# Hybrid encoder trunk on one core: the Hyena DFT in half blocks and plain float32

## The chip, the cores and the metric

The kernel runs on one core of a Trainium2 chip. The metric is device time in microseconds (us). PE is TensorE, with its weight loads as PEld; DVE is VectorE, ACT is ScalarE, POOL is GpSimd, and SP is SyncE, whose queue issues nearly all DMAs.

## What is computed

One layer of an encoder, for a prompt of 512 rows and a sample of 2048 rows of 1024 numbers. A normed input is projected onto three groups of heads (mLSTM, retention, Hyena), each is gated, and the output product and a final norm follow. The change touches only the Hyena group and its filters:

```python
def long_conv(u, spec, skip):
    l = u.shape[1]
    y = irfft(rfft(u, n=2 * l, axis=1) * spec[None], n=2 * l, axis=1)[:, :l]
    return y + u * skip

def hyena_branch(hy_in, hy_z, conv_w, conv_b, spec, skip):
    u = centred_conv3(hy_in, conv_w, conv_b)
    v, x1, x2 = split(u)                     # 512 channels each
    z = x1 * long_conv(v, spec[:, 0], skip[0])
    z = x2 * long_conv(z, spec[:, 1], skip[1])
    return z * silu(hy_z)
```

`spec` is the spectrum of a two-sided filter of the sequence's doubled length, made by a small sine network and a decay window, and normed by its absolute sum.

## The kernel before

A transform of length N (1024 or 4096) is two stages of matmuls. With n = 64 n1 + n2, the first stage (`stage_a0`, `stage_a`) transforms over n1, the second, one frequency k1 at a time (`freq`), over n2; the way back has the same two, the second of them in `inv_a`. Between the stages the data lie in DRAM (`Sg`, `F`, `Z`), since each stage has other numbers in its partitions. All tiles are 128 partitions by 512 channels.

Accuracy of float32 comes in one of two ways. `split` makes two float32r parts of an operand, a rounded one on ACT and a remainder on DVE or POOL, and `mm3` does three matmuls of parts. A matmul of float32 tiles needs no parts.

- **Stage over n1** (`stage_a`): the 128 partitions of a tile hold GS (the number of n2 values) interleaved short transforms; the matrix `ai` is 128x128 for each half h, block diagonal with interleaved blocks, so half of its rows are zero for a half h. Two `mm3` per tile, 20 tiles per order.
- **Frequency step** (`freq`): per k1 it loads a constant tile `cB` (forward and inverse matrix), a signal tile and a filter tile. `front` splits all three, `muls` does an `mm3` for each of signal and filter and swaps partition halves by DMAs, `mid` multiplies the complex numbers on DVE and POOL and splits the product, `back` does the `mm3` of the inverse. 40 steps per order, two orders.
- **Inverse stage** (`inv_a`): two loads, two splits and two `mm3` per tile that add into one PSUM tile; the gate product follows, and in order 0 at once the next order's `stage_a`.
- **Filters** (`filters`): per tile `first` (an `mm3`, the window), `product`, `total`/`second` (sums), `third` (a plain float32 matmul with the 128x128 matrix `fa`), `store`. 40 tiles per order.

The work around is woven in by hand: generators yield a cost on PE and a due time, and `merge` takes next the stream that is furthest behind its share (`lag` gives the due time). In the merge of `run`, the chain of Hyena stages runs beside the projections of the Hyena columns and the retention heads. `hb` is a ring of 9 tiles (HB), `hp` one of 16 (2 x HP) for parts; CB and FB are rings of constants and filter tiles. The mLSTM heads and the final product come behind. L numbers are lines of this kernel.

Of the kernel before, what the change touches and what calls it, by code (L numbers as in the profile page):

```python
# [39 lines left out]
HB, HP, CB, FB, B1, B2, KA, KB, KC, LS2, WF, VB, FH = 9, 8, 3, 3, 5, 6, 3, 3, 1, 3, 70, 4, 8  # L40
# [14 lines left out]
def fft_consts(L):  # L55
# [13 lines left out]
    FA = np.zeros((128, 128))  # L69
    for l in range(GF):  # L70
        FA[l::GF, l::GF] = A
    HG = GS // 2
    SA = np.zeros((128, 2, 128))
    IA = np.zeros((128, 2, 128))
    for h in range(2):
        for l in range(HG):
            n2l = h * HG + l
            SA[n2l::GS, h, l::HG] = A[:V]
            IA[l::HG, h, n2l::GS] = IAm
# [25 lines left out]
def constants():  # L105
    C = {'ident': np.eye(128, dtype=np.float32)}
    feats, tneg = [], []
    for L in (LP, LS):
# [9 lines left out]
        for j in range(NTF):  # L118
            n = 64 * (p // GF) + (p % GF) * (64 // GF) + j
# [27 lines left out]
class Trunk:  # L147
# [62 lines left out]
    def run(self):  # L210
        tc = self.tc
        with ExitStack() as ctx:
# [4 lines left out]
            with ExitStack() as c1:  # L217
# [5 lines left out]
                with tc.tile_pool(name="hy", bufs=2, side="right") as self.hy:  # L223
                    self.ai_of = (0, None)
                    self.drain(self.merge((self.chain(self.stage_a0(), self.freq(0), self.inv_a(0), self.freq(1), self.inv_a(1)), 270 * W3),
                                          (self.chain(self.projections(), self.retention()), 848)))
# [339 lines left out]
    def filter_setup(self):  # L566
# [4 lines left out]
        for L in (LP, LS):  # L571
            self.fa[L] = self.T(p0, [128, 128], f"FA{L}", bufs=1)
            nc.sync.dma_start(self.fa[L], C[f'FA{L}'])

    def filter_weights(self, o):
# [3 lines left out]
        raw, dl = self.T(p0, [128, 512], "fo"), self.T(p0, [128, 512], "dl", bufs=1)  # L579
# [42 lines left out]
    def filters(self, o):  # L622
# [11 lines left out]
        def first(n):  # L634
# [11 lines left out]
            if j == 0:  # L646
                sk[L] = self.T(p0, [128, 512], "fo")[0:1]
# [46 lines left out]

        n = len(seq)
        for i in range(n + 2):
            if i < n:
                first(i)
            if 0 <= i - 2:
# [6 lines left out]
            if 0 <= i - 2:  # L706
# [5 lines left out]
    def filter_mlp(self, i, blk):  # L712
# [20 lines left out]
        xv = x.rearrange("p (t c) -> p t c", t=4)  # L733
        outs = [(hd[0:64, :, 0:64], xv[0:64, :, 0:64]), (hd[64:128, :, 64:128], xv[64:128, :, 64:128])]
        if b == 0:
            outs.append((hd[64:128, 0, 0:1], xv[64:128, 0, 0:1]))
        self.sin(pm, outs, x, 128)
        if b == 0:
            nc.gpsimd.memset(hd[64:128, 0, 64:65], 0.0)
# [24 lines left out]
    def fetch_ai(self, L):  # L764

        if self.ai_of[0] != L:
            raw = self.hb().rearrange("p (a b) -> p a b", a=4)
            self.nc.sync.dma_start(raw, self.C[f'AI{L}'])
            self.ai_raw = (L, raw)

    def ai(self, L):

        if self.ai_of[0] != L:
            assert self.ai_raw[0] == L
            hl = [self.T(self.hy, [128, 4, 128], f"ai{i}", F32R, bufs=1) for i in range(2)]
            self.split(*hl, self.ai_raw[1])
            self.ai_of = (L, hl)
        return self.ai_of[1]
# [101 lines left out]
    def parts(self, t, eng=None):  # L880
        return self.split(*(self.T(self.hy, [128, 512], "hp", F32R, bufs=HP) for _ in range(2)), t, eng=eng)

    def stage_a0(self):
# [3 lines left out]
        def load(i):  # L887
            L, j = seq[i]
            st[i] = self.hb(self.X[0][L][j])

        n = len(seq)
        self.fetch_ai(LP)
        load(0)
        load(1)
        for i in range(n + 1):
            if i:
                L, j = seq[i - 1]
                self.stage_a(L, 0, j, st.pop(i - 1))
                if i < n and seq[i][0] != L:
                    self.fetch_ai(seq[i][0])  # L900
            if i < n:
                st[i] = self.parts(st[i])
                self.ai(seq[i][0])
            if i + 2 < n:
                load(i + 2)
            yield self.lag(1.28, 2.0)
# [12 lines left out]
    def freq(self, o):  # L919
# [5 lines left out]
        raw, As, Cs, X, Y = {}, {}, {}, {}, {}  # L925

        def load(i):
            L, k = seq[i]
            c = self.T(hy, [128, 256], "cB", bufs=1)
# [7 lines left out]
        def front(i):  # L937
            c, a, f = raw.pop(i)
            Cs[i] = self.split(*[self.T(hy, [128, 256], f"cB{x}", F32R, bufs=CB) for x in range(2)], c, eng=nc.gpsimd)
            As[i] = self.parts(a), self.parts(f, nc.gpsimd)  # L940

        def muls(i):

            (a, f), c, k = As.pop(i), [x[:, 0:128] for x in Cs[i]], seq[i][1]
# [6 lines left out]
            self.mm3(pf, c, f)  # L951
# [12 lines left out]
        def mid(i):  # L964
# [20 lines left out]
        for i in range(-1, n + 1):  # L985
            if i + 1 < n:
                front(i + 1)
# [14 lines left out]
    def inv_a(self, o):  # L1002
# [4 lines left out]
        def load(i):  # L1007
            L, j = seq[i]
            zs[i] = [self.hb(self.Z[L, o][:, 32 * h + j:32 * h + 32:geo(L)['NTS'], :]) for h in range(2)]

        def load_x(i):
            L, j = seq[i]
            xs[i] = self.hb(self.X[o + 1][L][j]), self.hb(self.hyg[SEQ0[L] + j:SEQ0[L] + L:geo(L)['NTS'], :]) if o == 1 else None

        def front(i):
# [717 lines left out]
```

## Time and profile before

| | |
|---|---|
| runs | 2694.83, 2703.0, 2709.08 us, median 2703.0 |
| profiled execution | 2704.09 us, span 2702.3 us |
| mean granted TensorE clock | 0.98 of full speed |
| DMA | 364.24 MB, mean 135 GB/s |
| instructions | 47221, of them 17590 matmuls |

The span is from the first to the last instruction. An engine's busy time is the sum of the stretches in which it has work; matmuls overlap in the pipeline and their ends are modelled, so a record's duration is longer than the distance to the next one's start. A wait is put down to the instruction that ended it.

### The profile page before, as it was taken

Reading aid. Unit: us, or ns where it says so; the run is one execution under the profiler, and the core shown is the slowest. Engines: PE = TensorE matmul, PEld = TensorE weight load, DVE = VectorE, ACT = ScalarE, POOL = GpSimd, SP = SyncE. Lnnn points to the kernel's source line nnn. Section 1 sums busy time; section 2 is a strip of 40 time slices with the busy share of each in tenths; the row PEclk is TensorE's granted clock in tenths of the full one; section 3 lists DMA queues with packets and bytes.
Section 4 is the critical chain, followed back from the end, with each engine's and each line's share of the span. In section 5 each row is a group of like instructions: output and inputs, shape, how many; then the busy total and the mean of one; then the engine's idle time right before and its main releaser. Section 6 shows DMA issues by size and latency. Waiting matters only on the chain.

```text
span 2702.3 us, 47221 instructions
## 1 busy us (share of the span) xinstructions
PE 2550.8 (94%) x17590; PEld 1918.7 (71%) x17590; DVE 1624.9 (60%) x3316; ACT 1355.3 (50%) x2626; POOL 758.4 (28%) x847
## 2 busy tenths in 40 slices
PE   7999989989989999999899999999999999899998
PEld 5566655545546787877777886787787877788887
DVE  7865546787786565577676666556565555522222
ACT  6455556665656455566666443454554545411111
POOL 0102322464443322456556352011011111100000
PEclk9999989999999999999999999999999999999999
DMA  5232266666667465566665665122122132322321
GB/s 203 83 109 100 94 194 223 212 206 178 191 189 205 136 202 179 146 177 184 174 176 172 178 218 152 36 47 72 40 64 56 45 97 63 122 104 106 110 98 51
DMA packets 266797, 364.24 MB, mean 135 GB/s; under 512 B 25382, under 2 KB 138814, under 8 KB 266568
## 3 DMA queue, kind: packets, MB, share of 16 engines
q1 hardware_dynamic: 266488, 360.98, 44.5%
q8 instruction: 138, 2.26, 0.3%
q14 instruction: 91, 0.75, 0.1%
q0 software_dynamic: 80, 0.26, 0.0%
HBM read 206.33 MB, written 112.89 MB: 118 GB/s over the span
## 4 chain that ended last, share of the span: by engine, by line
PE 62%; DMA 9%; DVE 9%; ACT 7%; issue 4%; POOL 2%; SPq 1%; POOLq 0%; DVEq 0%; ACTq 0%
PE ps L550 21%; PE ps L1284 12%; PE ps L540 11%; DMA rb<-rowd 3%; PE ps L372 3%; DMA hb<-hb 2%; PE ps L373 2%; PE ps L374 2%; PE ps L685 2%; DVE hb L968 1%; ACT hp L365 1%; POOL hb L967 1%; PE ps L1435 1%; PE ps L1272 1%; DMA hb<-Z 1%
## 5 line engine op out<-in xcount | busy, mean ns | idle before, releaser
L550 PE MATMUL ps<-whi,h 128*128 128x256 f16 (+2 forms) x6080 | 935.0, 258 | 0.1
L550 PEld LDWEIGHTS <-h 128*128 128x128 f16 x9120 | 775.8, 98 | 144.4 <-issue 59.7
L550 PE MATMUL ps<-wlo,h 128*128 128x256 f16 (+2 forms) x3040 | 739.3, 258 | 4.4 <-DVE wlo L523 4.4
L540 PE MATMUL ps<-h,whi 128*128 128x512 f16 x1600 | 491.1, 386 | 4.1 <-ACT whi L522 4.1
L365 ACT ACTIVATE hp<-hb 128x512 fp32r<-128x512 f32 x360 | 216.8, 626 | 252.5 <-DVE hb L968 139.7
L540 PE MATMUL ps<-h,wlo 128*128 128x512 f16 x800 | 306.2, 383 | 0.0
L540 PEld LDWEIGHTS <-whi 128*128 128x128 f16 x1600 | 153.9, 99 | 195.1 <-issue 51.0
L366 DVE TENSOR_TENSOR hp<-hb,hp 128x512 fp32r<-128x512 f32 x280 | 219.3, 795 | 76.1 <-ACT hp L365 72.7
L1284 PE MATMUL ps<-h,yh 128*128 128x512 f32 x760 | 210.4, 396 | 1.6 <-ACT yh L365 1.6
L1284 PEld LDWEIGHTS ps<-h,yh 128*128 128x128 f32 x760 | 141.7, 188 | 33.5 <-ACT yh L365 1.9
L366 POOL TENSOR_TENSOR hp<-hb,hp 128x512 fp32r<-128x512 f32 x80 | 114.8, 1435 | 168.4 <-ACT hp L365 159.7
L664 POOL TENSOR_TENSOR acc<-acc,win 128x512 f32<-128x512 f32 x80 | 108.3, 1354 | 175.3 <-ACT win L663 174.3
L540 PEld LDWEIGHTS <-wlo 128*128 128x128 f16 x800 | 79.1, 99 | 97.3 <-issue 12.4
L967 POOL TENSOR_TENSOR hb<-hb,hb 128x512 f32<-128x512 f32 x80 | 114.5, 1431 | 100.9 <-DMA hb<-hb 63.4
L372 PE MATMUL ps<-hp,cB 128*128 128x512 f32 x240 | 115.8, 484 | 26.0 <-ACT hp L365 25.3
L1615 POOL TENSOR_TENSOR m<-raw,tb 128x256 f32<-128x256 f32 x80 | 74.7, 934 | 181.5 <-ACT raw L1612 136.1
L1284 PE MATMUL ps<-h,yl 128*128 128x512 f32 x380 | 121.1, 396 | 0.0
L966 DVE TENSOR_TENSOR hb<-hb,hb 128x512 f32<-128x512 f32 x80 | 71.2, 890 | 75.5 <-DMA hb<-hb 66.4
L373 PE MATMUL ps<-hp,cB 128*128 128x512 f32 x240 | 105.9, 441 | 10.0 <-DVE hp L366 9.1
L800 DVE SCALAR_TENSOR_TENSOR cv<-u,sw,cv 128x512 f32<-128x512 f32 x120 | 107.1, 901 | 0.7
L968 DVE SCALAR_TENSOR_TENSOR hb<-hb,sgn,hb 128x512 f32<-128x512 f32 x80 | 81.6, 1020 | 38.6 <-POOL hb L967 35.5
L1349 POOL TENSOR_TENSOR ss<-ss,mhalf 128x1 f32<-128x1 f32 x20 | 10.9, 543 | 331.4 <-DVE ss L1348 328.8
(329 smaller groups left out, 4858.6 us busy)
## 6 DMA issues: line engine op xcount, KB each, us to landing
hb<-hb SPq DMA_DIRECT2D x316, 128.0 KB
F<-fo SPq DMA_DIRECT2D x80, 256.0 KB
Sg<-hb SPq DMA_DIRECT2D x80, 256.0 KB
hb<-Sg SPq DMA_DIRECT2D x80, 256.0 KB
hb<-F SPq DMA_DIRECT2D x80, 256.0 KB
Z<-hb SPq DMA_DIRECT2D x80, 256.0 KB
hb<-Z SPq DMA_DIRECT2D x80, 256.0 KB
rb<-rowd SPq DMA_DIRECT2D x80, 256.0 KB
```

The costliest lines, as they stand in the source:

```text
L365: self.nc.scalar.activation(hi, src, AF.Copy)
L366: (eng or self.nc.vector).tensor_tensor(out=lo, in0=src, in1=hi.bitcast(F32), op=ALU.subtract)
L372: mm(out, w[0], x[0], start=start, stop=False)
L373: mm(out, w[0], x[1], start=False, stop=False)
L540: nc.tensor.matmul(out, w[x][:, k, wc:wc + 128], self.hT[b][y][:, k], start=(k == 0 and i == 0), stop=(k == 7 and i == 2))
L550: nc.tensor.matmul(out, self.hT[b][x][:, k, c * 128:(c + 1) * 128], w[y][:, k, wc:wc + n], start=(k == 0 and i == 0), stop=(k == 7 and i = ...
L664: nc.gpsimd.tensor_tensor(out=acc, in0=acc, in1=win, op=ALU.add)
L800: nc.vector.scalar_tensor_tensor(d, u[:, t:t + 512], w(t), d, op0=ALU.mult, op1=ALU.add)
L967: nc.gpsimd.tensor_tensor(out=xs, in0=xs, in1=fi, op=ALU.mult)
L968: nc.vector.scalar_tensor_tensor(x, xs, self.sgn, x, op0=ALU.mult, op1=ALU.add)
L1284: self.nc.tensor.matmul(self.pss[n], a[p], w[q][:, n * 512:(n + 1) * 512], start=(k == 0 and i == 0), stop=(k == 11 and i == 2))
L1615: nc.gpsimd.tensor_tensor(out=m, in0=raw[:, :, ::-1], in1=sin[:, c:c + 2], op=ALU.mult)
```

## The change

The interleaved blocks of the short transforms are put one behind the other, so that each half of the partitions is a block of its own. The two matmuls of the forward stage then contract over 64 partitions each, the two of the inverse stage give 64 output rows each into the two halves of one PSUM tile, and `third` does two tiles at a time as four products of 64 rows and 64 columns. All of these, and the three matmuls of a frequency step, take float32 tiles as they are: `parts`, the `hp` tiles and the split constants go. Loads and stores whose rows have the new order are issued as two DMAs of 64 partitions. The stage matrices of both lengths are loaded once (`load_ai`). HB goes from 9 to 18, CB from 3 to 4, FB from 3 to 4, `fo` gets three buffers, and the planner's costs of the stages are lower. The rest of the diff, left out here, permutes the constants (`fft_consts`, the filter's sample order and its masks) to fit.

```diff
-HB, HP, CB, FB, B1, B2, ... = 9, 8, 3, 3, 5, 6, ...
+HB, CB, FB, B1, B2, ... = 18, 4, 4, 5, 6, ...
...
-                    self.drain(self.merge((self.chain(self.stage_a0(), ..., self.inv_a(1)), 270 * W3),
+                    self.load_ai()
+                    self.drain(self.merge((self.chain(self.stage_a0(), ..., self.inv_a(1)), 236 * W3),
...
         def third(n):
             L = seq[n][0]
-            ps = self.ps()
-            nc.tensor.matmul(ps, fa[L], st[n], start=True, stop=True)
+            ps = [self.ps(), self.ps()]
+            for i, m in enumerate((n, n - 1)):
+                for h in range(2):
+                    r = slice(64 * h, 64 * h + 64)
+                    nc.tensor.matmul(ps[h][64 * i:64 * i + 64], fa[L][r], st[m][r], start=True, stop=True)
             st[n] = ps
 
         def store(n):
-            fo = self.T(p0, [128, 512], "fo")
-            nc.vector.tensor_copy(fo, st.pop(n))
-            nc.sync.dma_start(self.F[L, o][:, j::g['NTF'], :], fo)
+            st.pop(n - 1)
+            for h, ps in enumerate(st.pop(n)):
+                fo = self.T(p0, [128, 512], "fo", bufs=3)
+                nc.vector.tensor_copy(fo, ps)
+                for i in range(2):
+                    nc.sync.dma_start(self.F[L, o][:, 32 * h + j + i:32 * h + 32:g['NTF'], :], fo[64 * i:64 * i + 64])
...
-            if 0 <= i - 2:
+            if 0 <= i - 2 and i % 2:
                 third(i - 2)
...
+    def load_ai(self):
+        self.ai = {L: self.T(self.hy, [128, 192], f"ai{L}", bufs=1) for L in (LP, LS)}
+        for L in (LP, LS):
+            self.nc.sync.dma_start(self.ai[L], self.C[f'AI{L}'])
+    def half_rows(x, L, j):
+        nt = geo(L)['NTS']
+        return x[SEQ0[L]:SEQ0[L] + L].rearrange("(q h t) c -> t h q c", h=2, t=nt)[j]
+    def in_halves(self, src):
+        t = self.hb()
+        for h in range(2):
+            self.nc.sync.dma_start(t[64 * h:64 * h + 64], src[h])
+        return t
+    def hx(self, i, L, j):
+        return self.in_halves(self.X[i][L][j].rearrange("(q h) c -> h q c", h=2))
...
     def stage_a(self, L, o, j, t):
-        ai = self.ai(L)
-        for h in range(2):
+        pss = [self.ps(), self.ps()]
+        for h, ps in enumerate(pss):
+            r = slice(64 * h, 64 * h + 64)
+            nc.tensor.matmul(ps, self.ai[L][r, 0:128], t[r], start=True, stop=True)
+        for h, ps in enumerate(pss):
             so = self.hb()
-            ps = self.ps()
-            self.mm3(ps, [a[:, h] for a in ai], t)
             nc.scalar.activation(so, ps, AF.Copy)
-            nc.sync.dma_start(self.Sg[L, o][:, 32 * h + j:32 * h + 32:nt, :], so)
+            nc.sync.dma_start(self.Sg[L, o][:, nt * h + j::2 * nt, :], so)
...
-        def front(i):
-            c, a, f = raw.pop(i)
-            Cs[i] = self.split(..., c, eng=nc.gpsimd)
-            As[i] = self.parts(a), self.parts(f, nc.gpsimd)
         def muls(i):
-            self.mm3(px, c, a)
+            nc.tensor.matmul(px, c[:, 0:128], a, start=True, stop=True)
...
-            self.mm3(pf, c, f)
+            nc.tensor.matmul(pf, c[:, 0:128], f, start=True, stop=True)
...
-            Y[i] = self.parts(x)
+            Y[i] = x
         def back(i):
-            self.mm3(pz, [x[:, 128:256] for x in Cs.pop(i)], Y.pop(i))
+            nc.tensor.matmul(pz, Cs.pop(i)[:, 128:256], Y.pop(i), start=True, stop=True)
...
         def mid(i):
             for h in range(2):
-                self.mm3(ps, [a[:, 2 + h] for a in ai], z[h], start=(h == 0), stop=(h == 1))
+                nc.tensor.matmul(ps[64 * h:64 * h + 64], self.ai[L][:, 128:192], z[h], start=True, stop=True)
             nc.vector.tensor_tensor(out=x, in0=x, in1=ps, op=ALU.mult)
             if o == 0:
-                st[i] = self.parts(x)
+                st[i] = x
             else:
                 nc.gpsimd.tensor_tensor(out=g, in0=g, in1=x, op=ALU.mult)
-                nc.sync.dma_start(self.ymix[r0 + j:r0 + L:nt, 1024:1536], g)
+                rows = self.half_rows(self.ymix[:, 1024:1536], L, j)
+                for h in range(2):
+                    nc.sync.dma_start(rows[h], g[64 * h:64 * h + 64])
```

## Rows read from the trace of the kernel before

**Rows 1.** The page's busy time, share of the span and instructions by engine.
```profile
PE 2550.8 (94%) x17590; PEld 1918.7 (71%) x17590; DVE 1624.9 (60%) x3316; ACT 1355.3 (50%) x2626; POOL 758.4 (28%) x847
```
**Rows 2.** The page's chain that ended last, share of the span by engine.
```profile
PE 62%; DMA 9%; DVE 9%; ACT 7%; issue 4%; POOL 2%; SPq 1%; POOLq 0%; DVEq 0%; ACTq 0%
```
**Rows 3.** Busy time by stretch; behind the engines clock, DMA share, GB/s.
```profile
core 0: us, PE busy (x) PEld busy (x) DVE busy (x) ACT busy (x) POOL busy (x), PEclk, DMA share, GB/s
350.00:1640.00 1290.00, 1196.29 (x8042) 882.47 (x8040) 877.68 (x1553) 755.43 (x1514) 581.32 (x541) 0.97 0.63 188
...
750.00:900.00 150.00, 132.81 (x759) 85.86 (x759) 107.03 (x168) 92.82 (x177) 67.08 (x68) 0.94 0.68 192
```
**Rows 4.** PE's waits from 350 to 1640 us: total, times, longest.
```profile
PE ps L372 <- ACT hp L365: 30.4, 23, 4.5
...
PE ps L373 <- DVE hp L366: 9.1, 14, 1.6
...
PE ps L374 <- DVE ai L366: 2.5, 1, 2.5
```
**Rows 5.** Timeline of PE, one `mm3` of a frequency step: start, us, what.
```profile
699.62 0.39 PE L372 MATMUL ps<-hp,cB 128*128 128x512 f32 x1
...
700.32 0.18 PE L550 MATMUL ps<-whi,h 128*128 128x16 f16 x1
```
**Rows 6.** Groups of matmuls, shapes apart: busy us, mean ns, idle before.
```profile
L372 PE MATMUL ps<-hp,cB 128*128 128x512 f32 x240 | 115.8, 484 | 26.0 <-ACT hp L365 25.3 <-ACT hb L976 0.7
L373 PE MATMUL ps<-hp,cB 128*128 128x512 f32 x240 | 105.9, 441 | 10.0 <-DVE hp L366 9.1 <-POOL hp L366 0.9
L374 PE MATMUL ps<-hp,cB 128*128 128x512 f32 x240 | 95.2, 397 | 0.0
L685 PE MATMUL ps<-f,FA 128*128 128x512 f32 x160 | 83.1, 602 | 2.5 <-DVE sw L761 2.5
L372 PE MATMUL ps<-hp,ai 128*128 128x512 f32 x160 | 69.8, 455 | 5.3 <-ACT hp L365 5.3
L373 PE MATMUL ps<-hp,ai 128*128 128x512 f32 x160 | 67.0, 419 | 0.0
L374 PE MATMUL ps<-hp,ai 128*128 128x512 f32 x160 | 63.7, 398 | 2.5 <-DVE ai L366 2.5
```
**Rows 7.** Timeline of PE, one plain float32 matmul of `third`.
```profile
248.19 1.02 PE L685 MATMUL ps<-f,FA 128*128 128x512 f32 x2
249.05 0.27 PE L550 MATMUL ps<-whi,h 128*128 128x256 f16 x1
```
**Rows 8.** Timeline of PE around matmuls with fewer rows or columns (rows*columns).
```profile
76.95 0.27 PE L550 MATMUL ps<-whi,h 128*128 128x256 f16 x1
77.06 0.60 PE L436 MATMUL ps<-ident,xt 128*128 128x128 f32 x4
77.59 1.12 PE L727 MATMUL ps<-h,w 64*128 64x512 f32 x2
78.64 0.28 PE L550 MATMUL ps<-whi,h 128*128 128x256 f16 x1
...
93.07 1.93 PE L719 MATMUL ps<-ft,w 33*64 33x512 f32 x4
94.92 0.33 PE L436 MATMUL ps<-ident,xt 128*128 128x128 f32 x1
```
**Rows 9.** Groups of the splits of `hp` and of the B constants.
```profile
L365 ACT ACTIVATE hp<-hb 128x512 fp32r<-128x512 f32 x360 | 216.8, 626 | 252.5 <-DVE hb L968 139.7
L366 DVE TENSOR_TENSOR hp<-hb,hp 128x512 fp32r<-128x512 f32 x280 | 219.3, 795 | 76.1 <-ACT hp L365 72.7
L366 POOL TENSOR_TENSOR hp<-hb,hp 128x512 fp32r<-128x512 f32 x80 | 114.8, 1435 | 168.4 <-ACT hp L365 159.7
...
L366 POOL TENSOR_TENSOR cB<-cB,cB 128x256 fp32r<-128x256 f32 x80 | 73.4, 917 | 46.2 <-ACT cB L365 45.2 <-PE ps L372 0.9
```
**Rows 10.** SP's DMAs of `hb`: issue ns min/median/max, first and last start; waiters, us.
```profile
L877 SPq DMA_DIRECT2D hb<-X x60: 319/424/1555, 368.8 to 1640.7; - x60
...
  POOL hb L967: 63.4, 41
```

More of the change, by code (lines that the diff above doesn't have):

```diff
@@ L68, in fft_consts @@
     IAm[1] = (-1.0) ** n1v
[L69 to L74, printed above, removed]
+    HF, HG = GF // 2, GS // 2
+    FA = np.zeros((128, 64))
+    SA = np.zeros((128, 128))
+    IA = np.zeros((128, 64))
     for h in range(2):
+        for l in range(HF):
+            FA[64 * h + l:64 * h + 64:HF, l::HF] = A
         for l in range(HG):
-            n2l = h * HG + l
-            SA[n2l::GS, h, l::HG] = A[:V]
-            IA[l::HG, h, n2l::GS] = IAm
+            SA[64 * h + l:64 * h + 64:HG, l::HG] = A[:V]
+    for l in range(HG):
+        IA[l::HG, l::HG] = IAm
     n2 = np.arange(64)[:, None]
@@ L705, in filters @@
                 second(i - 1)
-            if 0 <= i - 2:
+            if 0 <= i - 2 and i % 2:
                 store(i - 2)
@@ L762, in hyena_scale @@
         self.scaled.add(o)
[L764 to L778, printed above, removed]
+    def load_ai(self):
+        self.ai = {L: self.T(self.hy, [128, 192], f"ai{L}", bufs=1) for L in (LP, LS)}
+        for L in (LP, LS):
+            self.nc.sync.dma_start(self.ai[L], self.C[f'AI{L}'])
+    @staticmethod
+    def half_rows(x, L, j):
[6 more added lines that the diff above has]
+        return t
     def halo_blocks(self, pool, blocks, tag):
@@ L878, in hb @@
         return t
-    def parts(self, t, eng=None):
-        return self.split(*(self.T(self.hy, [128, 512], "hp", F32R, bufs=HP) for _ in range(2)), t, eng=eng)
+    def hx(self, i, L, j):
+        return self.in_halves(self.X[i][L][j].rearrange("(q h) c -> h q c", h=2))
     def stage_a0(self):
@@ L898, in stage_a0 @@
                 self.stage_a(L, 0, j, st.pop(i - 1))
[L899 to L903, printed above, removed]
             if i + 2 < n:
                 load(i + 2)
-            yield self.lag(1.28, 2.0)
+            yield self.lag(0.86, 1.5)
     def stage_a(self, L, o, j, t):
@@ L935, in load_filter, with muls @@
             raw[i][2] = self.hb(V[L][1][k])
-        def front(i):
+        def muls(i):
             c, a, f = raw.pop(i)
-            Cs[i] = self.split(*[self.T(hy, [128, 256], f"cB{x}", F32R, bufs=CB) for x in range(2)], c, eng=nc.gpsimd)
-            As[i] = self.parts(a), self.parts(f, nc.gpsimd)
-        def muls(i):
-            (a, f), c, k = As.pop(i), [x[:, 0:128] for x in Cs[i]], seq[i][1]
+            Cs[i], k = c, seq[i][1]
             x, xs, fr, fi = (self.hb() for _ in range(4))
             px, pf = self.ps(), self.ps()
-            self.mm3(px, c, a)
+            nc.tensor.matmul(px, c[:, 0:128], a, start=True, stop=True)
             nc.scalar.activation(x, px, AF.Copy)
@@ L1008, in load @@
             L, j = seq[i]
-            zs[i] = [self.hb(self.Z[L, o][:, 32 * h + j:32 * h + 32:geo(L)['NTS'], :]) for h in range(2)]
+            zs[i] = [self.hb(self.Z[L, o][:, geo(L)['NTS'] * h + j::2 * geo(L)['NTS'], :]) for h in range(2)]
         def load_x(i):
             L, j = seq[i]
-            xs[i] = self.hb(self.X[o + 1][L][j]), self.hb(self.hyg[SEQ0[L] + j:SEQ0[L] + L:geo(L)['NTS'], :]) if o == 1 else None
-        def front(i):
-            zs[i] = [self.parts(z) for z in zs[i]]
+            g = self.in_halves(self.half_rows(self.hyg, L, j)) if o == 1 else None
+            xs[i] = self.hx(o + 1, L, j), g
         def mid(i):
@@ L1046, in inv_a @@
                 load_x(i + 1)
-                front(i + 1)
-                self.fetch_ai(seq[i + 1][0])
             if i + 2 < n:
                 load(i + 2)
-            yield self.lag(2.56 if o == 0 else 1.28, LI)
+            yield self.lag(1.71 if o == 0 else 0.86, LI)
     def gates(self):
```

32 lines of the change are left out of this document (13 added, 19 removed).

## The prediction

> **What bounds the kernel now.** I read the page's first block, then the chain, then the stretches of time, then PE's groups and waits. The busy shares [rows 1] say that PE (TensorE) is at work 94% of the span and no other engine over 60%. PE's shares come from modelled ends, so the chain is asked next: 62% of what ended last is PE, and DMA, DVE and ACT have 9, 9 and 7% [rows 2]. The last loads of the edited code start at about 1640 us [rows 10]; the mLSTM heads and the final product behind it keep their instructions. In the stretch from 350 to 1640 us PE is busy 1196.3 of 1290 us and idle 93.7, with DVE, ACT and POOL at 68, 59 and 45% and the DMA engines at 0.63 [rows 3]. So PE work that is added there lengthens the run nearly one for one, and work taken from the other engines pays only through PE's idle time. Of that, 42 us are waits for the two parts into which operands are split (30.4, 9.1 and 2.5) [rows 4]; some 51 are waits for other things.
>
> **PE time before.** An operand in parts costs three float32r matmuls (`mm3`). In a clean stretch they start 0.23 us apart, 0.70 for the three [rows 5]. Their mean records are longer than the clean 397 ns: 484, 441 and 397 in the frequency steps, 455, 419 and 398 in the DFT stages [rows 6]. I take the surplus, 0.13 and 0.08 us per `mm3`, as bubbles behind the two waits and as time at the lower clock. A frequency step has three `mm3`: 240 x 0.83 = 199, plus the idle of its rows, 26.0 + 10.0 [rows 6], is 235 us. The stages over n1, forward and inverse, have 160: 160 x 0.78 = 125, plus 5.3 + 2.5 idle, is 133 us. The filters' `third` (L685) is a plain float32 matmul already. It shows as two records, and from its first start to the next instruction pass 0.86 us [rows 7]; 80 of them, with 2.5 idle, are 71 us. Together 439 us.
>
> **Frequency steps after.** Each of 240 `mm3` becomes one plain float32 matmul of full size: 240 x 0.86 = 206 us. The waits for parts go; what is late next is the operand itself (the DVE add of L968, or a load). I leave 8 of the 36 us of idle for that: 214 us, 21 less than before. The bounds are 0 and all 36 left, so 206 to 242: the sign of this part is not safe either.
>
> **Stages and `third` after.** The forward stage is two matmuls with 64 rows of contraction each, on partitions 0 to 63 and 64 to 127; the inverse is two with 64 output columns each; `third` does four quarter-size matmuls for two tiles at once. Streaming is still 512 elements, four passes. No row of before shows two matmuls in different parts of the array, but three lines use one part. L727 (64 rows) holds PE 1.05 us to the next start against 0.86 for a full one, so 0.19 is added; and before it four L436 records took 0.53 us, where 0.11 each would be 0.44: about 0.10 for emptying the array [rows 8]. L719 (33 rows, 64 columns) ran four records in 1.85 us, which is 4 x 0.43 + 0.13 [rows 8]. So a visit to a part of the array costs about 0.29 us with 128 columns of weights and 0.25 with 64, once per visit and not per matmul. The page TensorEngine Tiling (Array Packing) of the Trainium skill, under Key Properties, says that changing the tiling mode drains TensorE, which speaks against many short visits; these rows agree, at some 0.1 us on entering.
>
> What the halves then cost depends on whether they run side by side. Lower bound: all side by side, one matmul's 0.86 for the pair or the four. Upper bound: one after the other, as L719's records, which lie on one part, do. I take a value between. Records start in program order, and a float32 matmul is two records with different weights in the same part. So the second record of the first half must start before the first record of the second half: in a pair only the middle can overlap, three steps of 0.43 for four records, and five steps for `third`'s eight.
> - one after the other: 2.01 (forward), 1.97 (inverse), 3.69 us (`third`, per two tiles); 40 of each: 307 us
> - overlap in the middle: 1.58, 1.54, 2.40; 40 of each: 221 us
> - all side by side: 1.15, 1.11, 1.11; 40 of each: 135 us
>
> Before, these were 133 + 71 = 204. With 3 us of waits left they change by +106, +20 and -66.
>
> **What the other engines give back.** Removed are 360 ACT splits (216.8 us), 280 DVE and 80 POOL subtractions (219.3 and 114.8), and 80 splits of the B constants (73.4 on POOL; ACT's share of those is extra) [rows 9]. That is 25% of DVE's work in the stretch and about 30% of ACT's and of POOL's [rows 3]. If the 51 us of other waits shrink by 30%, PE gets 16 us; bounds 0 and 51, the latter only if every such wait were for a split.
>
> **DMAs and queues.** Bytes stay the same but for the small A constants, now loaded once. The halves make some 160 more issues on SP's queue: 20 for the first stage's loads, 40 for the X loads, 20 for gates, 20 for ymix, 80 for the F stores. At 0.42 us each (the median for a load of X [rows 10]) that is 67 us on a queue spread over the whole hyena part. In-order SP is where it would hurt: behind these issues stand the swaps between partition halves that L967 and L966 wait for (63.4 us on POOL [rows 10]). The number of `hb` buffers goes from 9 to 18, but the 16 `hp` buffers go, and loads now stay in `hb` until their matmul. I price this at nothing, covered by two iterations of lookahead; if the cover is gone, 160 x 0.42 is the bound. POOL and ACT issue none of it. `store` still makes one DVE copy per tile, but now of two in a row; the next `product` stands behind them by one copy more, which the filters' lag covers.
>
> **The sum**, against the profiled execution's 2704.1 us (1.1 above the median of the runs): -21 + 20 - 16 = -17, so 2687 there and **2686 us** beside the median.
>
> **Rivals.** About 0.5%, 13.5 us, is what a measurement of this kernel can tell from no change.
> 1. Overlap in the middle, as above: 2686. For it: records start in order in every row. Against: no row of before shows any overlap between parts. Chance 0.55. Its own range is 2650 to 2730 (other waits 0 to 51, frequency waits 0 to 36); about half of it is faster, three tenths the same, two tenths slower.
> 2. No overlap at all: -21 + 106 - 16 = +69, **2772 us**, slower. The mechanism is one: the second half waits until the first has left the array, in 80 stage visits and 40 visits of `third`. It decides as soon as more than about a third of the step between 20 and 106 is real (+47 makes it 10 us slower, +50 passes 13.5). For it: L719's records, and the emptying that the visits already show. Chance 0.25.
> 3. Halves fully side by side: -21 - 66 - 16 = -103, **2600 us**. This needs the first records of both halves to start together, before the second record of the first. Against it stands the order of starts in all rows. Chance 0.14. The page TensorE: Matmul & The Clock Gate, Part 3, states that matmuls on distinct row or column groups run at once, starting some 4 ns apart, and that they start and end in strict order. No run here shows the first yet; by its span model alone it would be this case, by its order it is case 1.
> 4. A lower clock: the granted clock is 0.97 over the stretch and 0.94 from 750 to 900 us, where PE was busy 89% [rows 3]. A mean of 0.97 is 6% of the time at 1.2 GHz instead of 2.4, a loss of 39 us in 1290. If array parts and drains count as idleness and double that, case 1 becomes 2725, slower. From 0.95 on it is felt. The loss of the splits' waits speaks against. Chance 0.06; a late swap behind the extra SP issues would look alike and is held in it.
>
> **How the numbers follow.** The time is that of case 1. The range reaches to case 3 and past case 2, **2600 to 2780**, which leaves out some 2 in 10 (the far half of case 3, case 2 with all waits kept). Faster: 0.28 of case 1, 0.14 of case 3, 0.01 of case 2: 0.43. Same: 0.16 + 0.02 + 0.01 = 0.19. Slower: 0.11 + 0.22 + 0.05 = 0.38.
>
> **What would show it.** In the changed kernel's frequency rows, pairs of records 0.43 apart, busy sums near 206 us, and PE waits on L968 or loads below 10 us in all: right. In the stage rows, the start of the second half's first record: just behind the second record of the first half is case 1, 0.43 or more later case 2, beside the very first record case 3. Spacing from the first stage record to the next foreign instruction, 1.6, 2.0 or 1.15, prices it. For `third`, eight records within 2.4, 3.7 or 1.1 us. The other-waits share: PE idle in the hyena stretch down from 93.7 to about 40. The forecast is wrong as a whole if PE idle stays, because then a DMA chain (swap, DVE, matmul) and not PE sets the frequency steps, or if the clock's share falls below 0.95.

## The result and the profile after

The changed kernel takes 2643.43 us (median of four runs, 2636.32 to 2651.88) against 2703.02: the ratio is 0.9772 [0.975, 0.9794], 60 us faster. The profiled execution is the fastest of the four, 2636.32 us, 67.8 less than the one profiled before. The forecast was 2686, so the sign was right and the gain more than three times as large; the time lies within the range.

The page of the kernel after, its busy time by engine and its chain by engine, answers to [rows 1] and [rows 2]:

```profile
span 2634.6 us, 45835 instructions
...
PE 2518.7 (96%) x17350; PEld 1795.0 (68%) x17350; DVE 1358.7 (52%) x3032; ACT 1141.9 (43%) x2182; POOL 555.4 (21%) x687
...
PE 51%; DMA 5%; DVE 4%; ACT 2%; issue 1%; POOL 1%; SPq 1%; POOLq 0%; DVEq 0%; ACTq 0%
```

The shares of the chain after add up to 65%: it could be followed back only to about 920 us, so it leaves out half of the Hyena part and isn't to be compared with the one before share by share. PE lost 32 us of busy time and 36 us of idle time. DVE, ACT and POOL lost 266, 213 and 203 us; none of them was the bound, so what that was worth has to be tested.

The Hyena part ends earlier now, so its stretch is cut at 1570 us instead of 1640 (columns as in [rows 3]):

```profile
350.00:1570.00 1220.00, 1166.96 (x7674) 764.14 (x7672) 614.74 (x1266) 537.15 (x1063) 376.87 (x381) 0.98 0.68 198
...
750.00:900.00 150.00, 140.40 (x851) 90.49 (x848) 64.86 (x125) 56.42 (x105) 31.55 (x39) 0.97 0.64 180
```

PE is idle 53.0 of 1220 us, where it was 93.7 of 1290 [rows 3]. In the stretch from 750 to 900 us the granted clock rose from 0.94 to 0.97. The four longest of PE's waits from 350 to 1570 us:

```profile
PE ps L974 <- DVE hb L968: 11.1, 7, 2.6
PE ps L917 <- DMA hb<-X: 7.3, 1, 7.3
PE ps L372 <- ACT w L365: 5.6, 1, 5.6
PE ps L842 <- DVE cv L809: 5.4, 2, 4.7
```

The waits for parts [rows 4] are gone but for the filter's own. In a frequency step the product of L968 is late now, as named, by 11.1 us in all. The changed matmuls, grouped with shapes apart (columns as in [rows 6]):

```profile
L974 PE MATMUL ps<-hb,cB 128*128 128x512 f32 x160 | 85.8, 619 | 11.1 <-DVE hb L968 11.1
L947 PE MATMUL ps<-hb,cB 128*128 128x512 f32 x160 | 82.2, 596 | 0.0
L951 PE MATMUL ps<-hb,cB 128*128 128x512 f32 x160 | 81.7, 592 | 0.0
L917 PE MATMUL ps<-hb,ai 64*128 64x512 f32 x160 | 49.9, 676 | 7.3 <-DMA hb<-X 7.3
L689 PE MATMUL ps<-f,FA 64*64 64x512 f32 x320 | 45.3, 615 | 0.0
L1019 PE MATMUL ps<-hb,ai 128*64 128x512 f32 x160 | 44.2, 618 | 0.0
```

The count and the mean of a row already speak: 320 records of `third` at a mean of 615 ns would be 197 us if each had its own time, and the union of their spans is 45.3. They lie on top of each other. The timeline of PE shows how. First a `third` for two tiles (four matmuls, eight records), then an inverse stage:

```profile
278.63 0.40 PE L373 MATMUL ps<-w,hd 128*128 128x512 f32 x1
278.86 0.40 PE L374 MATMUL ps<-w,hd 128*128 128x512 f32 x1
279.19 1.09 PE L689 MATMUL ps<-f,FA 64*64 64x512 f32 x8
280.21 0.60 PE L540 MATMUL ps<-h,whi 128*128 128x512 f16 x2
...
1454.60 0.27 PE L550 MATMUL ps<-wlo,h 128*128 128x256 f16 x1
1454.71 0.27 PE L550 MATMUL ps<-whi,h 128*128 128x256 f16 x1
1454.91 1.08 PE L1019 MATMUL ps<-hb,ai 128*64 128x512 f32 x4
1455.92 0.60 PE L1680 MATMUL ps<-qkT 128*128 128x128 f32 x3
```

Eight records take 1.02 us to the next instruction's start, four of an inverse stage 1.01. Before `third` pass 0.33 us where these matmuls follow at 0.23 (278.63 to 278.86); before the inverse stage 0.20 against 0.11 (1454.60 to 1454.71). So entering costs 0.10 and 0.09 us. The next fence is one forward stage, the timeline asked three times: up to 408.692 us, up to 409.21, and whole. A row counts the records that had started by then.

```profile
408.69 0.69 PE L917 MATMUL ps<-hb,ai 64*128 64x512 f32 x1
...
408.69 0.70 PE L917 MATMUL ps<-hb,ai 64*128 64x512 f32 x2
...
408.69 1.13 PE L917 MATMUL ps<-hb,ai 64*128 64x512 f32 x4
409.75 0.49 PE L374 MATMUL ps<-w,hd 128*128 128x512 f32 x1
```

The start times in the trace, from the first: 0, 7, 534 and 540 ns, the next instruction at 1059. Those of `third`: 0, 7, 13, 20, then 480, 487, 493, 500. Only the two late records of the stage raise a semaphore, as the second record of a lone matmul does, so the first two are the first records of the two halves. Of the 36 forward stages whose four records stand together, 35 show the same steps within 1 ns. So all halves start their first record 7 ns apart, and then all their second ones. That is the sign that the prediction gave to case 3, "all side by side".

For a ledger, the time from the first matmul's start to the last one's is split in three. Idle time of PE is what the rows show ahead of a matmul [rows 6]; shorter stalls, which the modelled end of the record before covers, are not in it. Of the rest, half of what lies at the lower clock counts as lost there (a matmul of L540 takes 216 ns to the next start at 2.4 GHz and 427 ns at 1.2 GHz). What remains is called work.

| us | work | lost at the lower clock | idle | all |
|---|---|---|---|---|
| before | 2503.8 | 46.6 | 141.4 | 2691.9 |
| after | 2487.3 | 31.0 | 105.9 | 2624.2 |
| difference | -16.5 | -15.6 | -35.5 | -67.7 |

So only a fourth of what the profiled execution gained is TensorE's own work. That fourth is a sum of two parts of opposite sign, as `e1` (+23) and `e2` (-37) show below. Of the idle time, 36.0 us stood ahead of the frequency steps and 10.3 ahead of stages and `third` [rows 6]; now it is 11.1 and 7.3. Some 100 of the 120 visits to the smaller tiles come straight behind a full-size matmul, and entering them costs about 9 us in all (0.09 to 0.10 each); this is in the work after.

### The profile page after: what moved, and what is told of

It is laid out like the page before. It is cut to its first block, busy times and chain, and to the rows that moved or that the text cites. A ratio compares the mean times of both kernels' runs of the same rounds, so it can differ in the third digit from the quotient of the medians.

```text
span 2634.6 us, 45835 instructions
## 1 busy us (share of the span) xinstructions
PE 2518.7 (96%) x17350; PEld 1795.0 (68%) x17350; DVE 1358.7 (52%) x3032; ACT 1141.9 (43%) x2182; POOL 555.4 (21%) x687
## 4 chain that ended last, share of the span: by engine, by line
PE 51%; DMA 5%; DVE 4%; ACT 2%; issue 1%; POOL 1%; SPq 1%; POOLq 0%; DVEq 0%; ACTq 0%
PE ps L550 20%; PE ps L1278 13%; PE ps L540 5%; DMA rb<-rowd 3%; PE ps L1019 1%; DMA hb<-hb 1%; PE ps L951 1%; PE ps L947 1%; PE ps L1429 1%; PE ps L1630 1%; PE ps L974 1%; PE ps L1266 1%; DMA wraw<-in_w_in 1%; PE ps L1501 1%; PE ps L1689 1%
## 5 line engine op out<-in xcount | busy, mean ns | idle before, releaser
L550 PE MATMUL ps<-whi,h 128*128 128x256 f16 (+2 forms) x6080 | 917.5, 256 | 0.6 <-DVE Rb L1634 0.6
L540 PE MATMUL ps<-h,whi 128*128 128x512 f16 x1600 | 484.8, 383 | 5.9 <-ACT whi L522 4.5
L540 PE MATMUL ps<-h,wlo 128*128 128x512 f16 x800 | 305.2, 382 | 0.2 <-DVE wlo L523 0.2
L540 PEld LDWEIGHTS <-whi 128*128 128x128 f16 x1600 | 153.5, 99 | 211.7 <-issue 66.7
L540 PEld LDWEIGHTS <-wlo 128*128 128x128 f16 x800 | 78.8, 98 | 96.5 <-issue 6.4
L966 DVE TENSOR_TENSOR hb<-hb,hb 128x512 f32<-128x512 f32 x80 | 57.5, 719 | 158.3 <-DMA hb<-hb 150.0
L968 DVE SCALAR_TENSOR_TENSOR hb<-hb,sgn,hb 128x512 f32<-128x512 f32 x80 | 72.5, 907 | 60.0 <-POOL hb L967 49.9
L809 DVE SCALAR_TENSOR_TENSOR cv<-u,sw,cv 128x512 f32<-128x512 f32 x120 | 99.3, 846 | 1.2
L1606 ACT ACTIVATE raw<-ps,winv 128x256 f32<-128x256 f32 x80 | 37.9, 473 | 140.9 <-PE ps L550 92.9
L974 PE MATMUL ps<-hb,cB 128*128 128x512 f32 x160 | 85.8, 619 | 11.1 <-DVE hb L968 11.1
L523 DVE SCALAR_TENSOR_TENSOR wlo<-wraw,wsc,whi 128x512 f16<-128x512 f32 (+2 forms) x116 | 84.5, 763 | 22.1 <-ACT whi L522 21.0
L658 DVE TENSOR_TENSOR f<-ps,win 128x512 f32<-128x512 f32 x80 | 54.7, 687 | 73.6 <-PE ps L374 51.6
L1334 DVE TENSOR_TENSOR xt<-xt,ps 128x512 f32<-128x512 f32 x40 | 25.8, 684 | 126.9 <-PE ps L1278 126.9
L1341 ACT ACTIVATE sq<-xt 128x1024 bf16<-128x1024 f32 x19 | 20.1, 1058 | 160.4 <-DVE xt L1334 160.4
```

Source lines behind the costliest of these rows:

```text
L523: v = nc.vector.scalar_tensor_tensor(lo[:, k], raw[:, k], s, hi[:, k], op0=ALU.mult, op1=ALU.subtract)
L540: nc.tensor.matmul(out, w[x][:, k, wc:wc + 128], self.hT[b][y][:, k], start=(k == 0 and i == 0), stop=(k == 7 and i == 2))
L550: nc.tensor.matmul(out, self.hT[b][x][:, k, c * 128:(c + 1) * 128], w[y][:, k, wc:wc + n], start=(k == 0 and i == 0), stop=(k == 7 and i = ...
L658: nc.vector.tensor_tensor(out=f, in0=ps, in1=win, op=ALU.mult)
L809: nc.vector.scalar_tensor_tensor(d, u[:, t:t + 512], w(t), d, op0=ALU.mult, op1=ALU.add)
L966: nc.vector.tensor_tensor(out=x, in0=x, in1=fr, op=ALU.mult)
```

## The experiments

**The theories.** A: the gain is TensorE's own time, because halves run side by side. B: it is work taken from ACT, DVE and POOL, which no longer make PE wait. Later ones, about the planner's costs above all, are stated with the runs. Each ratio is against the kernel before, timed on the same chip. Work, lower clock and idle time of a run are those of the ledger, for its profiled execution.

### The two parts of the change, each alone

`e1` is the kernel before with frequency steps as plain float32 matmuls (and `hb` 11, `hp` 7, CB 4).

```diff
-            self.mm3(px, c, a)
+            nc.tensor.matmul(px, c[:, 0:128], a, start=True, stop=True)
...
-            if i + 1 < n:
-                front(i + 1)
```

> The kernel before with the frequency steps alone in plain float32 (hb ring 11, hp ring 7); stages over n1 and third as before. Theory A (TensorE time decides): the 240 mm3 of these steps took 226 us from start to next start, 240 x 0.86 = 206 us replace them, so about -19 us, 2684 us, ratio 0.993. Theory B (the relief of ScalarE, VectorE and GpSimd decides, two thirds of which lies here): about two thirds of the 60 us gained, -40 us, 2663 us, ratio 0.985.

2671.34 us, 0.9883 [0.986, 0.9906]: 32 us faster, between the two. The ledger decides for B: against the kernel before, TensorE's work rises by 23 us (to 2527.2), idle time falls by 41 (to 100.3), 27 of it ahead of the frequency steps (36.0 to 8.9), and 20 less are lost at the lower clock (26.4). The 226 us of theory A were distances between starts, with stalls and time of other matmuls in them.

`e2` is the changed kernel with the frequency steps in parts again (`hb` 10, `hp` 8).

```diff
-            nc.tensor.matmul(px, c[:, 0:128], a, start=True, stop=True)
+            self.mm3(px, c, a)
```

> The changed kernel with the frequency steps in parts again (hb ring 10, hp ring 8); stages over n1 and third in half blocks. Theory A: 2643 + 19 = 2662 us, ratio 0.985. Theory B: a third of the gain is left, 2683 us, ratio 0.993.

2701.21 us, 0.9982 [0.9965, 0.9999]. Both missed: the blocks alone gave next to nothing, though they take 37 us off TensorE's work (to 2467.2). Idle time rises by 24 us (to 165.5) and the loss at the lower clock by 6. PE's two longest waits from 350 to 1640 us, and ACT's longest:

```profile
PE ps L372 <- ACT hp L365: 34.6, 24, 4.3
PE ps L373 <- DVE hp L366: 9.7, 16, 1.6
...
ACT hp L365 <- DVE hb L975: 172.5, 69, 6.1
```

Most of what the blocks save is given back in waits. ACT stands 172.5 us in front of the rounding of the product (139.7 before [rows 9]). Two explanations were open: that split, and the planner's lower costs. They are taken up below.

### Is it side by side, and what does it need?

`e3` keeps everything plain float32 but makes every stage matmul 128 x 128 again, with zeros in the other half.

```diff
-            r = slice(64 * h, 64 * h + 64)
-            nc.tensor.matmul(ps, self.ai[L][r, 0:128], t[r], start=True, stop=True)
+            nc.tensor.matmul(ps, self.ai[L][:, h], t, start=True, stop=True)
```

> The changed kernel with every half or quarter matmul of the stages and of third replaced by a full-size plain float32 one with zero-padded matrices, same results, hb ring 17; nothing can run side by side. Theory A: 120 pairs of visits at about 1.19 us with emptying (143 us) become 120 x 1.72 = 206 us, +63 us, 2706 us, ratio 1.001. Theory B (side by side is not decisive): within +20 us of the changed kernel, 2643 to 2663 us, ratio 0.978 to 0.985.

2694.46 us, 0.9969 [0.9957, 0.9981]: 51 us slower than the changed kernel, with 65 us more work (2552.2) and about the same idle time (99.2), so A is right on this. Its groups, beside L917, L689 and L1019 above:

```profile
L913 PE MATMUL ps<-hb,ai 128*128 128x512 f32 x160 | 82.1, 637 | 11.0 <-DMA hb<-X 6.8 <-DVE hb L1016 4.2
L686 PE MATMUL ps<-f,FA 128*128 128x512 f32 x160 | 78.0, 606 | 0.6 <-ACT u L793 0.5
L1015 PE MATMUL ps<-hb,ai 128*128 128x512 f32 x160 | 76.2, 599 | 0.0
```

The mean of a record hardly differs, the union does: 82.1 for 49.9, 76.2 for 44.2. Without the halves plain float32 in these stages costs work: 25 us more than in `e1`, which leaves them in parts.

`e7` puts one 128 x 128 transpose between the two halves of each forward stage.

```diff
             nc.tensor.matmul(ps, self.ai[L][r, 0:128], t[r], start=True, stop=True)
+            if h == 0:
+                nc.tensor.transpose(self.ps()[:, 0:128], self.ident, self.ident)
```

> The changed kernel with a full-size transpose, read by nobody, between the two half matmuls of the forward stage (40 tiles). If halves run side by side only when next to each other: each half costs 0.86 + 0.29 and the transpose 0.11, 2.41 instead of 1.16 us a tile, 40 x 1.25 = +50 us, 2693 us. If a half is taken up past the foreign instruction: +5 us, 2648 us.

2689.86 us, 0.9942 [0.9922, 0.9962], 46 us slower than the changed kernel. Its timeline, whole and (last row) up to 452.21 us:

```profile
451.68 1.12 PE L917 MATMUL ps<-hb,ai 64*128 64x512 f32 x2
452.73 0.33 PE L919 MATMUL ps<-ident 128*128 128x128 f32 x1
452.99 1.12 PE L917 MATMUL ps<-hb,ai 64*128 64x512 f32 x2
454.04 0.60 PE L540 MATMUL ps<-h,whi 128*128 128x512 f16 x2
...
451.68 0.69 PE L917 MATMUL ps<-hb,ai 64*128 64x512 f32 x1
```

Each half takes 1.05 us alone, the tile 2.36 instead of 1.06: 40 x 1.30 = 52 us. With a full-size matmul between them in PE's queue the halves do not overlap. A foreign matmul that itself uses only a part of the array was not tried.

### What the other engines' work was worth

`e5` gives the changed kernel a ring of 11 `hb` tiles instead of 18.

```diff
-HB, CB, ... = 18, 4, ...
+HB, CB, ... = 11, 4, ...
```

> The changed kernel with 11 hb tiles instead of 18. If the ring is worth nothing (the prediction's price): 2643 us within 10, ratio 0.978. If lookahead of the loads carries part of the gain: 2660 us or more, ratio from 0.984.

2640.57 us, 0.9767 [0.9748, 0.9786]: the larger ring is worth nothing.

`e4` and `e6` put all 360 splits back on the changed kernel, but nobody reads the parts; PE's work stays that of the change. `e4` has room for two `hp` tiles and 16 `hb`, `e6` for eight and 11.

```diff
+    def parts(self, t, eng=None):
+        self.split(*(self.T(self.hy, [128, 512], "hp", F32R, bufs=HP) for _ in range(2)), t, eng=eng)
...
+            self.parts(a)
+            self.parts(f, nc.gpsimd)
...
+            self.parts(x)
```

> The changed kernel with the removed splits of signal and filter tiles done again on ScalarE, VectorE and GpSimd into two tiles that nobody reads (360, 280 and 80 operations; the splits of the B constants are left out), hb ring 16; matmuls stay plain. Theory A: at most +10 us, 2643 to 2653 us, ratio 0.978 to 0.982. The 16 us of the prediction for the relief: 2659 us, ratio 0.984. Theory B: +40 us or more, 2683 us, ratio 0.993.

> The run before this one (11 hb tiles) plus the idle splits of signal and filter tiles, now into a ring of 8 tiles as the kernel before had, not 2. If the 91 us of the first run with idle splits came from its ring of 2 tiles, which queues ScalarE behind each subtraction: at most 16 us over the run with 11 tiles. If the work on ScalarE, VectorE and GpSimd itself costs that much: 40 us or more over it.

`e4` took 2733.92 us, 1.0116 [1.0092, 1.014], `e6` 2719.42, 1.0056 [1.0037, 1.0074], 79 us over `e5`. The ring explains little of that (0.6%, some 15 us, between the two); idle splits cost more than the whole change had brought. Against `e5`, `e6` has 56 us more idle time of PE, 19 more lost at the lower clock and 11 more work. ACT's longest waits in `e6`, from 350 to 1640 us:

```profile
ACT hp L365 <- DVE hb L974: 218.7, 71, 11.1
ACT hp L365 <- DMA hb<-Z: 63.6, 29, 6.0
```

ACT stands idle in front of a split whose operand is late, and the theory (H in the texts below) is that what comes next in its queue, evictions of PSUM among it, is held up behind it. To separate this standing from the work itself, the splits should read a tile that is always there. `e9` let them read a constant tile:

```diff
+        self.split(*(self.T(self.hy, [128, 512], "hp", F32R, bufs=HP) for _ in range(2)), self.res, eng=eng)
```

> As the run with idle splits and a ring of 8 (11 hb tiles, same 360, 280 and 80 operations at the same places), but all of them read one tile that is set once at the start, so none waits for an operand. Theory W (the work on the three engines costs): 2719 us as there. Theory H (ScalarE runs its queue in order and stands at a split whose operand is late, with other streams' work behind it): at most 20 us over the 2641 us of the run with 11 hb tiles.

2744.63 us, 1.0158 [1.0133, 1.0183], which doesn't answer the question. The group of the idle roundings (count, ns, first and last start) shows why: without an operand to wait for they were scheduled ahead, and all had run by 850 us.

```profile
L365 ACT ACTIVATE hp<-res x360: 612/623/677, 365.6 to 850.5; 128x512 fp32r<-128x512 f32 x180
```

`e13` is the same with these instructions held at their place in the program.

```diff
+        self.tc.keep_in_program_order(self.nc.scalar.activation(hi, self.res, AF.Copy))
```

> Idle splits of the tile set once, as before (360, 280 and 80 operations, 11 hb tiles, ring of 8), but each kept at its place in program order, since the run with the resident tile had them all done by 850 us. Theory W (work on the three engines, spread out, costs): 2719 us, as with late operands. Theory H (standing at late operands costs): at most 2675 us.

2684.56 us, 0.9935 [0.9912, 0.9959]: 44 us over `e5`. So neither theory is right alone: the work, on engines that are busy 57% (ACT) and 67% (DVE) of the stretch, costs 44 us. The other 35 up to the 79 go with late operands, but `e6` also differs in that its splits are not held at their place. Between the profiled executions of `e13` and `e5` lie 50 us: 22 are idle time of PE (130.5 for 108.7), 16 the lower clock and 12 work.

`e10` adds the split of the product alone (80 on ACT, 80 on DVE, read by nobody).

```diff
             nc.vector.scalar_tensor_tensor(x, xs, self.sgn, x, op0=ALU.mult, op1=ALU.add)
+            self.parts(x)
```

> The changed kernel with 11 hb tiles and idle splits of the frequency steps' product alone (80 on ScalarE, 80 on VectorE), the one split whose operand comes at the end of the chain swap, GpSimd, VectorE. Theory H: a large part of the 79 us, 2665 to 2700 us. Theory W: a fifth of the work, a fifth of the price, 2657 us.

2673.58 us, 0.9888 [0.9866, 0.9911]: 33 us over `e5`, for ACT's group of 50.4 us of work:

```profile
L365 ACT ACTIVATE hp<-hb 128x512 fp32r<-128x512 f32 x80 | 50.4, 630 | 230.9 <-DVE hb L971 230.8
```

`e11` and `e12` test the same place from the other side: the kernel before and `e2`, with the product's rounding on DVE, which made the product, instead of ACT.

```diff
-            Y[i] = self.parts(x)
+            hi, lo = (self.T(hy, [128, 512], "hp", F32R, bufs=HP) for _ in range(2))
+            nc.vector.tensor_copy(hi, x)
+            nc.vector.tensor_tensor(out=lo, in0=x, in1=hi.bitcast(F32), op=ALU.subtract)
+            Y[i] = hi, lo
```

> The kernel before with the rounded part of the frequency steps' product made on VectorE, right behind the instruction that makes the product, instead of on ScalarE; nothing else. Theory H: ScalarE no longer stands at it (139.7 us of waits), 2675 to 2690 us. Theory W: the same work on the busier engine, 2703 us or more.

> The run with blocks only and parts in the frequency steps, with the same move of the product's rounding to VectorE. Theory H: the gain of the blocks shows at last, 2660 to 2685 us. Theory W: 2701 us or more.

`e11`: 2685.32 us, 0.9938 [0.9916, 0.996], 17 us faster than before; `e12`: 2694.8, 0.9966 [0.9953, 0.998], 6 us faster than `e2`. In `e11` ACT's wait for the product is gone, and its longest is now 63.5 us:

```profile
ACT cB L365 <- PE ps L373: 63.5, 40, 6.3
```

So more than a fourth of the whole gain could be had in the kernel before, by moving 80 instructions to the engine that makes their operand. The 6 us of `e12` are not clear of noise, so this place alone did not explain `e2`: in `e12` PE waits for the product's parts instead.

```profile
PE ps L372 <- DVE hp L977: 40.1, 20, 4.7
```

### The planner's costs

`e15` is `e2`, and `e14` the changed kernel, with the costs that the kernel before gives its stages.

```diff
-self.inv_a(1)), 236 * W3),
+self.inv_a(1)), 270 * W3),
...
-            yield self.lag(0.86, 1.5)
+            yield self.lag(1.28, 2.0)
...
-            yield self.lag(1.71 if o == 0 else 0.86, LI)
+            yield self.lag(2.56 if o == 0 else 1.28, LI)
```

> Blocks only, parts in the frequency steps, with the planner's costs of before. If the lower costs drove the Hyena chain into its splits and so hid the gain of the blocks: 2670 to 2690 us. If the splits' work and waits take it whatever the order: 2695 to 2703 us, as with the new costs.

> The changed kernel with the planner's costs of before (1.28 and 2.0 for the first stage, 2.56 and 1.28 for the inverse, 270 for the chain). If the costs are worth nothing: 2643 us within 10, ratio 0.978. If they carry part of the gain: 2655 us or more.

`e15`: 2678.55 us, 0.9916 [0.9895, 0.9937], 23 us faster than `e2`. The lower costs had hidden the gain of the blocks. The two do the same work (2467.8 and 2467.2 us); `e15` is idle 13 us less. PE's waits for parts in `e15`, to be set beside `e2`'s:

```profile
PE ps L372 <- ACT hp L365: 24.1, 20, 4.0
PE ps L373 <- DVE hp L366: 10.4, 15, 2.0
```

`e14`: 2634.03 us, 0.9745 [0.9719, 0.977]; 9 us faster than the changed kernel, but the intervals overlap.

With old costs throughout there is a table of two by two: plain frequency steps alone -1.17% (`e1`), blocks alone -0.84% (`e15`), both -2.55% (`e14`). Both give 0.54% (some 0.4 either way), about 15 us, more than the sum.

The last four kernels look for more. `e8` makes the filter's `first` a plain float32 matmul too; `e16` adds true costs of a frequency step to that (0.86 and 1.71, total 288), `e17` the old costs of the stages, `e18` both.

```diff
-            self.mm3(ps, [x[:, t] for x in hids[i]], w3)
+            nc.tensor.matmul(ps, hids[i][:, t], w3, start=True, stop=True)
...
-                yield self.lag(0.64, LF)
+                yield self.lag(0.86, LF)
```

> The changed kernel with the filters' first product (80 mm3, 78 us from start to next start, and 10.5 us of waits for its parts) in plain float32 too; its two splits go. If plain float32 pays where parts bring waits: 80 x 0.86 = 69 us and the waits gone, -10 to -25 us, 2618 to 2633 us, ratio 0.969 to 0.974. If four passes for three cost more than the waits: 2643 to 2655 us.

> The changed kernel with the filters' first product in plain float32, and with planner costs for the frequency steps that match what they take of TensorE (0.86 and 1.71 for 0.64 and 1.28, chain 288). A better spread of the remaining waits: 2625 to 2638 us, ratio 0.972 to 0.976, under the changed kernel's. If the order is not what is left: 2639 to 2648 us.

> The changed kernel with the filters' first product in plain float32 and with the planner's costs of before (270 for the chain). The two gains add if they come from different waits: -5 and -9 us on 2643, 2629 us, ratio 0.9725. If both come from the same waits: 2634 to 2639 us.

> As the run before this one, and the frequency steps' costs at 0.86 and 1.71 as well (chain 322). If costs nearer to what the steps need keep helping: 2620 to 2630 us, ratio 0.970 to 0.973. If not: as the run before, 2629 to 2634 us.

| | us | ratio |
|---|---|---|
| `e8` | 2638.69 | 0.9758 [0.9736, 0.9781] |
| `e16` | 2631.7 | 0.974 [0.9719, 0.9761] |
| `e17` | 2634.18 | 0.9757 [0.9733, 0.978] |
| `e18` | 2644.08 | 0.9786 [0.976, 0.9812] |

None of them is told apart from the changed kernel for certain. `e16` has the lowest time of all, and its interval still touches. In `e8` TensorE's work rises by 15 us, and idle time and the lower clock together give back 16. `e18` is 10 us above `e17`, but their intervals overlap.

## Why the prediction was wrong

**The step that failed** is the choice of case 1: "a float32 matmul is two records with different weights in the same part. So the second record of the first half must start before the first record of the second half". The trace after shows the opposite: 0, 7, 534, 540 ns. The 120 visits were put at 221 us; without idle time they took 131, and about 9 for entering. Program order holds for the instructions, not for their records. The prices given to case 3 were right to 0.01: 1.15, 1.11 and 1.11 us a visit forecast, 1.06, 1.01 and 1.02 measured to the next start plus 0.10 for emptying. No row of before could show this, as was said; but the rule that spoke for it was at hand and was read as if it spoke of records. The page TensorE: Matmul & The Clock Gate of the Trainium skill, Part 3, lets matmuls on distinct row or column groups start some 4 ns apart and gives the span as one duration plus that; here it is 7 ns, and for float32 the whole of it holds twice, once for each record.

The time alone could not have told the cases apart: with the frequency waits and the other waits all gone, case 1 comes to 2643 us by its own terms (the text gives 2650). The start times do.

**A second step failed**, the work of before: "I take the surplus, 0.13 and 0.08 us per `mm3`, as bubbles behind the two waits and as time at the lower clock". The means are long largely for another reason. A float32r matmul behind a matmul of another kind is shown to start about 28 ns after that one's start, while the other still runs:

```profile
693.44 0.38 PE L540 MATMUL ps<-h,wlo 128*128 128x512 f16 x1
693.47 0.58 PE L372 MATMUL ps<-hp,cB 128*128 128x512 f32 x1
693.89 0.60 PE L540 MATMUL ps<-h,whi 128*128 128x512 f16 x2
```

The two take 0.45 us, which is 0.22 and 0.23; the record of 0.58 us holds time of the matmul before it. By `e1`, 240 plain matmuls (206 us) are 23 us more work than 240 `mm3`, so these took about 183 us and not 199.

**Case 3's sum** was -103 and the profiled execution gained 68:

- TensorE's work was to fall by 52 us: +7 in the frequency steps, -59 in the stages and `third`. It fell by 16.5: `e1` has +23 for the first, `e2` and `e15` -37 and -36 for the second.
- Idle time ahead of the changed matmuls was to fall by 35 and fell by 28; ahead of all others by 16, and it fell by 8.
- The lower clock was priced at nothing in this case and gave 16.

Luck has a part in the sign that was forecast: with the work of before sized right, case 1 would have come to about 16 us slower, not 17 faster (an estimate from `e1`, `e2` and the 140 us of the visits). The overlap that it denied made up for that.

**The frequency steps**: -21 was forecast, as 7 more work and 28 less idle time. `e1` shows 23 and 27, so on TensorE the two nearly cancel; what `e1` gains lies in other idle time (-14) and the lower clock (-20). In the changed kernel 11.1 us of waits are left, forecast 8 (the sign asked for below 10), on the line named. PE idle in the stretch was to fall to about 40; it is 53.0. The busy sum was to show near 206 us; the rows show 249.7, since records are longer than the distance of their starts. Without idle time these distances add up to 205.4, so the sign was named for the wrong view.

**The relief** was mis-sized in kind. Idle splits cost 44 to 79 us, the product's alone 33, moving 80 roundings gave 17, and in `e1`, where only the frequency steps lose their parts, idle time and the lower clock give 61. But it is no term to be added. The blocks alone take 36 us off TensorE's work in `e15` and shorten the run by 24, with 11 us more idle time. PE's waits for the parts are not longer there (34.5 us, 39.5 before [rows 4]); new are waits for loads (8.7 and 6.5 us). With plain frequency steps (`e14` against `e1`) the blocks take off 41 us of work and 37 of the run. Why less idle time goes with less time at the lower clock in most of these runs was not separated; `e7` has little idle time (102.4) and loses 41 us there.

**The planner's costs** were listed in the change and not priced. They cost 23 us where splits are still there and between nothing and some 16 in the changed kernel (0.9772 and 0.9745 with their intervals). How they do it is only argued: a lower cost lets other streams move ahead of the Hyena chain or it ahead of them, and `e2` waits 10 us longer for parts than `e15`. Their profiled executions lie 15 us apart, 13 of it idle time; the rest of the 23 stays open.

**Priced at nothing, nearly rightly:** SP's extra issues (in the stretch PE waits once, 7.3 us, for a load of X, where before it waited for none; no run tests them alone), and rightly the larger ring (`e5`). **The lower clock** of rival 4 went the other way, from a mean of 0.980 to 0.986. Three slips change nothing: the listed issues add up to 180, not 160 (the trace has 178 more); a visit with 64 columns adds 0.23 us by its rows (0.13 + 0.10), not 0.25; and the `hp` ring has 8 tiles, since both parts share it, not 16.

## What to carry to other kernels

Two matmuls that use half of the array each and stand next to each other on different rows or columns cost little more than one, in float32 too (1.06 us and 0.10 for entering, against 0.86); look for matrices with structural zeros, order the data so that the zeros become whole halves, and keep full-size matmuls out from between. A plain float32 matmul is more work than three of parts, and can still pay by the waits and the splits that go. Price work on an engine that is not the bound by what it stands in front of in its queue: 80 splits of an operand that arrives late cost 33 us, and moving their rounding to the engine that makes the operand gave 17 us in the kernel before. Whoever cuts the work of a planned stream must look at the plan's costs as well, and time them apart. Read the gain of a matmul from a run's sums of work, lower clock and idle time, not from mean records.

## What the hardware showed that was not expected

- The two records of float32 matmuls on different parts of the array interleave: first, first, second, second, with 7 ns between neighbours and about 0.5 us between the pairs. Four quarter-size matmuls (eight records) take 1.02 us, one full-size matmul 0.86 [rows 7].
- A full-size matmul between two halves undoes it: 2.36 instead of 1.06 us a tile.
- Entering the smaller tiles costs 0.09 to 0.10 us ahead of the visit. The page TensorEngine Tiling (Array Packing) of the Trainium skill, Key Properties, says that a change of the mode drains TensorE; that agrees, and some 100 entries make 9 us of it.
- A plain float32 matmul is more work than three float32r matmuls of parts (0.86 against 0.70 us without waits [rows 5, 7]; 23 us for 240 of them in `e1`) and still made the run 32 us shorter.
- A float32r matmul behind one of another kind has its start recorded about 28 ns after that one's start, so its record holds time of the matmul before it.
